# Split fp32r sums over 64 channels, and intra-chunk products of two heads as one group, in a hybrid RWKV-7 and attention layer

## The chip, the cores and the metric

The kernel runs on one core of a Trainium2 chip. The metric is the device time of one execution in microseconds. The five engines work through instruction queues of their own, each in a fixed order: PE (TensorE, matrix products), DVE (VectorE), ACT (ScalarE), POOL (GpSimd) and SP (which here issues the transfers).

## The reference

One layer of a streaming encoder, on 1,024 frames of a prompt and 64 frames of a second sequence with a cache of 256 (D_MODEL 1024, 8 RWKV heads and 8 attention heads of 64 channels):

```python
h = _rms_norm(x, norm1_g) * (1 + sc1[:, None]) + sh1[:, None]
proj = h @ w_in
...
kk = kk / jnp.maximum(jnp.linalg.norm(kk, axis=-1, keepdims=True), 1e-12)
...
y, s_new = _rwkv_scan(rh, _heads(decay, RWKV_HEADS), kh, vh, kk, _heads(a, RWKV_HEADS), s_prev.astype(f32))
mu = jnp.mean(y, axis=-1, keepdims=True)
var = jnp.mean(jnp.square(y - mu), axis=-1, keepdims=True)
y = ((y - mu) * lax.rsqrt(var + GN_EPS)).reshape(b, t, RWKV_WIDTH) * gn_g + gn_b
bonus = (jnp.sum(rh * kh * r_k, axis=-1, keepdims=True) * vh).reshape(b, t, RWKV_WIDTH)
...
q = _rms_norm(_heads(q, FOX_HEADS), fox_q_g)
kf = _rms_norm(_heads(kf, FOX_HEADS), fox_k_g)
...
mix = jnp.concatenate([y_rwkv, y_fox], axis=-1) @ w_out
x = x + gt1[:, None] * mix
...
ffn = (jax.nn.silu(h2 @ w_ffn_gate) * (h2 @ w_ffn_up)) @ w_ffn_down
```

Every norm, mean and sum over the last axis of a head is a sum over 64 channels.

## The kernel before, in words

Data lies with channels on the 128 partitions, two heads of 64 channels to a tile, and frames along the columns. The frames come in two halves: half 0 has 512 frames (8 chunks of 64), half 1 has the other 512 and the 64 of the second sequence (9 chunks, 576 columns, worked on in two pieces of 288).

For each half a table of letters (ORDER) sets in which order the work is written down. Z, Q, K and V are projections (`pmm`, lines 321 to 323: each weight and each activation is split into a high and a low part in the type fp32r, and three products are summed). D and A prepare a pair of heads j for the scan; B (rwkv_b) is the scan over its 8 or 9 chunks; N (rwkv_n) normalises the scan's result y; q and k (fox_norm) normalise the queries and keys of attention. A scheduler then fixes each engine's order, once, from dependencies and estimated times; on the chip an engine never overtakes in its queue.

A step of the scan is a chain: pR (L624) on PE, copies of it on DVE and ACT (L626, L627), pSA (L637), its negation on DVE and ACT (L638, L639), pS (L640), the new state on DVE (L644), and the next step's pR. The two pY products (L635, L645) stand beside it.

The sums over 64 channels are made by bsum (L398): the data are multiplied on PE by a 128x128 matrix with a block of ones (`bones`) or of 1/64 (`bmean`) for each head, in fp32, one product (`pbs`, L402) to a piece of 512 columns in half 0 and 288 in half 1. There are 48 calls, 24 in each half: for each pair two in A, two in N, one for q and one for k. The intra-chunk products pA (L491) multiply kb by rk for each chunk and head, 64 rows by 128 columns, four chunks to a PSUM tile of tag "ra"; a masked eviction on DVE (L493) makes At of them, from which the next steps (pg, pw, pu, lines 550 to 578) form the inverse matrices.

SBUF is handed out by tags, each with a number of buffers. `slot` without a tag takes from "ms", which has one buffer. "fx" has four: raw and squared q or k (fraw, fsq) hold two of them from their projection to the end of fox_norm.

Of the kernel before, what the change touches and what calls it, by code (L numbers as in the profile page):

```python
# [2 lines left out]

# [4 lines left out]
F32 = mybir.dt.float32  # L8
F32R = mybir.dt.float32r
BF16 = mybir.dt.bfloat16  # L10
AF = mybir.ActivationFunctionType
ALU = mybir.AluOpType
# [4 lines left out]
P = 128  # L17
# [3 lines left out]
SS = 64  # L21
# [43 lines left out]
class K:  # L65
    def __init__(self, tc, A, O):
        self.tc, self.nc, self.A, self.O = tc, tc.nc, A, O
        self.flip = 0

        self.pool_lo = False  # L70


    def consts(self):
# [39 lines left out]
    def consts2(self):  # L113
        nc, A = self.nc, self.A
        c, f = self.cpool, self.fper
        self.bones = f.tile([P, P], F32, name="bones")
        self.bmean = f.tile([P, P], F32, name="bmean")
        for t, v in ((self.bones, 1.0), (self.bmean, 1.0 / 64)):
            nc.gpsimd.memset(t, 0.0)
            nc.gpsimd.memset(t[0:64, 0:64], v)  # L120
            nc.gpsimd.memset(t[64:128, 64:128], v)
        self.tri = f.tile([P, P], F32, name="tri")
        nc.gpsimd.memset(self.tri, 1.0)
        nc.gpsimd.affine_select(out=self.tri, in_=self.tri, compare_op=ALU.is_ge, fill=0.0, base=0,
                                pattern=[[1, P]], channel_multiplier=-1)
        self.lacc = None


        self.amask = f.tile([P, 2, P], F32, name="amask")
        nc.gpsimd.memset(self.amask, 1.0)  # L130
        for h in range(2):
            am = self.amask[:, h]
            nc.gpsimd.memset(am[64 * h:64 * h + 64, 0:64], -1.0)
            for r in (0, 64):
                nc.gpsimd.affine_select(out=am[r:r + 64, 0:64], in_=am[r:r + 64, 0:64], compare_op=ALU.is_gt,
                                        fill=0.0, base=0, pattern=[[1, 64]], channel_multiplier=-1)
                nc.gpsimd.affine_select(out=am[r:r + 64, 64:128], in_=am[r:r + 64, 64:128], compare_op=ALU.is_ge,
                                        fill=0.0, base=0, pattern=[[1, 64]], channel_multiplier=-1)

        self.whi2 = [self.fper.tile([P, RW], F32R, name=f"whi{x}") for x in range(2)]
        self.wlo2 = [self.fper.tile([P, RW], F32R, name=f"wlo{x}") for x in range(2)]
        for x in range(2):
            raw = self.slot([P, RW], name="wlr")
            for r in (0, 64):
                nc.sync.dma_start(raw[r:r + 64], A["w_lora"][x])
            r = slice(64 * x, 64 * x + 64)
            nc.scalar.copy(self.whi2[x], raw)
            nc.gpsimd.memset(self.wlo2[x].bitcast(F32), 0.0)  # L150
            nc.vector.tensor_tensor(self.wlo2[x][r], raw[r], self.whi2[x][r].bitcast(F32), op=ALU.subtract)

        self.fb = c.tile([P, 8], F32, name="fb")
        nc.sync.dma_start(self.fb, A["fox_f_b"].to_broadcast([P, 8]))
        self.fsel = c.tile([P, 8], F32, name="fsel")
        nc.vector.tensor_reduce(self.fsel, self.ident.rearrange("p (i b) -> p b i", i=4)[:, 0:8], axis=AX.X, op=ALU.add)
        self.wg = self.fper.tile([P, RW], F32, name="wg")
        nc.sync.dma_start(self.wg, A["w_gate_up"])
        self.carry = c.tile([P, 14], F32, name="carry")
        self.ns = c.tile([P, 28], F32, name="ns")  # L160

        self.state = [f.tile([P, 64], F32, name=f"state{j}") for j in range(4)]
        for t in self.state:
            nc.gpsimd.memset(t, 0.0)

        self.cmul = f.tile([P, 320], F32, name="cmul")
        nc.gpsimd.memset(self.cmul, 1.0)
        nc.gpsimd.memset(self.cmul.rearrange("p (c t) -> p c t", t=64)[:, :, 0:1], 0.0)
# [227 lines left out]
            evac(ps[:, 0:n], off, n)  # L396

    def bsum(self, hf, w, x, evac, tag):  # L398
        nc = self.nc
        for off, n in hf.chunks:  # L400
            ps = self.ps([P, 512], tag=tag, name="pbs")
            nc.tensor.matmul(ps[:, 0:n], w, x[:, off:off + n], start=True, stop=True)  # L402
            evac(ps[:, 0:n], off, n)

    def split_lora(self, hf, z):

# [8 lines left out]
    def rwkv_d(self, hf, j, zl):  # L415

        nc, vc = self.nc, self.vc
        n, nch = hf.n, hf.nch
        col = lambda base: vc[:, base + j:base + j + 1]
        ch = lambda t: t[:, 0:n].rearrange("p (c t) -> p c t", t=64)  # L420
        sw, a = self.slot(name="sw", tag="sa"), self.slot(name="a", tag="sa")
        for off, m in hf.chunks:

            ps = [self.ps([P, 512], tag="ra", name="plora") for _ in range(2)]
            for x in range(2):
                nc.tensor.matmul(ps[x][:, 0:m], self.whi2[x][:, j * P:(j + 1) * P], zl[:, x, off:off + m], start=True,
                                 stop=False)
            for x in range(2):
                nc.tensor.matmul(ps[x][:, 0:m], self.wlo2[x][:, j * P:(j + 1) * P], zl[:, x, off:off + m], start=False,
                                 stop=True)  # L430
            for x, (dst, base) in enumerate(((sw, V_W0), (a, V_A0))):
                nc.vector.tensor_scalar(dst[:, off:off + m], ps[x][:, 0:m], col(base), -43.0, op0=ALU.add, op1=ALU.max)
        self.sigm(sw[:, 0:n], 1.0)
        self.sigm(a[:, 0:n], 1.0)
        cum = self.slot(name="cum", tag="sa")
        for o in range(0, n, 320):
            m = min(320, n - o)
            nc.vector.tensor_tensor_scan(cum[:, o:o + m], self.cmul[:, 0:m], sw[:, o:o + m], 0.0, ALU.mult, ALU.add)
        pp = self.pp
        nc.scalar.activation(pp[:, 0:nch, 1:65], ch(cum), AF.Exp, scale=-KAPPA)  # L440
        nc.scalar.activation(cum[:, 0:n], cum[:, 0:n], AF.Exp, scale=KAPPA)
        return a, cum

    def rwkv_a(self, hf, j, z, d):

        nc, vc, O = self.nc, self.vc, self.O
        n, nch = hf.n, hf.nch
        ng = 2 * nch
        col = lambda base: vc[:, base + j:base + j + 1]
# [34 lines left out]
        for c in range(0, nch, 4):  # L484
            m = min(4, nch - c)

            pa = [self.ps([P, 4, P], tag="ra", name="pA") for _ in range(2)]
            for i in range(m):
                for h in range(2):
                    hp = slice(64 * h, 64 * h + 64)  # L490
                    nc.tensor.matmul(pa[h][:, i], kb[hp, c + i], rk[hp, c + i], start=True, stop=True)  # L491
            for h in range(2):
                nc.vector.tensor_tensor(At[:, c:c + m, :, h], pa[h][:, 0:m].rearrange("p i (x t) -> p i x t", x=2),  # L493
                                        self.amask[:, h:h + 1].rearrange("p o (x t) -> p o x t", x=2)
                                        .to_broadcast([P, m, 2, 64]), op=ALU.mult)

        nb = 2 * ng
        dm = self.dpool.tile([2, ng, 2, 16, 16], F32, tag="dm", name="dm")
# [13 lines left out]
        for s in range(15):  # L512
            m = 15 - s
# [172 lines left out]
    def logf(self, hf):  # L686
# [58 lines left out]
            nc.gpsimd.tensor_copy(keep, acc)  # L745
            self.lacc = keep

        q4 = self.fpool.tile([P, 7, 4, 8], F32, tag="lq", name="lq")
        hi = self.fpool.tile([P, 7, 2, 8], F32R, tag="lh", name="lh")
        for i, _, _, _, _ in order:  # L750
            nc.vector.tensor_copy(hi[:, i, 0], pl[:, i])
# [85 lines left out]
    def by_tokens(self, hf, j, src):  # L837
        nc = self.nc
        pt = self.ps([P, 4, P], tag="fx", name="pkv")
        for i in range(4):  # L840
            nc.tensor.transpose(pt[:, i], src[:, i * P:(i + 1) * P], self.ident)
        dst, ds_ = self.slot([P, 4, P], name="tok", tag="fx"), None
        nc.scalar.copy(dst, pt)
        nc.sync.dma_start(self.O["fox_v"][j, :, 4 * hf.i:4 * hf.i + 4], dst)
        if hf.smp:
            pt = self.ps([SS, P], tag="fx", name="pkvs")
            nc.tensor.transpose(pt, src[:, 512:576], self.ident)
            ds_ = self.fpool.tile([SS, P], F32, tag="toks", name="toks")
            nc.scalar.copy(ds_, pt)
            nc.sync.dma_start(self.O["fox_v"][j, 0:SS, 8], ds_)  # L850
        return dst, ds_
# [518 lines left out]
    def run(self):  # L1370
        tc, nc, A, O = self.tc, self.nc, self.A, self.O
        halves = [Half(0), Half(1)]
        with ExitStack() as top:
# [22 lines left out]
            self.cmid = E(mid, "cmid")  # L1396
            self.consts()
            self.spool = MultiPool({"mrow": E(mid, "smrow", 2), "mred": E(mid, "smred", 2)})
            self.spool.pools.update({"ms": E(mid, "sms", 1)})
            hst = top.enter_context(ExitStack())  # L1400
            hp = E(hst, "hpool", side="right")
            self.hhi = hp.tile([P, KT, 576], F32R, name="hhi")
# [48 lines left out]
            RP = lambda p, tags: MultiPool({t: E(rws, p + t, b) for t, b in tags})  # L1451
            self.rpool.pools.update(RP("r", (("pp", 1), ("pb", 2), ("mb", 1), ("wb", 1), ("tb", 1), ("xl", 1))).pools)
            self.spool.pools.update(RP("s", (("sa", 4),)).pools)
            self.fpool = FP("f", (("toks", 1), ("lfu", 1), ("lfe", 1), ("lfw", 1), ("lacc", 2), ("lq", 1), ("lh", 1)))
            self.spool.pools.update(FP("s", (("fx", 4),)).pools)
            self.ops = {}

# [305 lines left out]
```

## Time and profile before

| | us |
|---|---|
| median of 3 runs (lowest to highest) | 1698.58 (1694.36 to 1699.02) |
| the profiled execution: its span | 1691.4 |
| PE busy in it | 1642.2 |
| weight loads of PE | 1438.5 |
| DVE busy | 1122.1 |
| ACT busy | 725.6 |

The page gives times of one profiled execution; its span is the time from its first instruction to its last, and the three runs were timed apart from it. Rows of a group read: line, engine, operation, tile written <- tiles read, how many records; then the busy time of the group in us and the mean of one in ns; then the idle time of the engine before it and who ended it. Rows of the timeline read: start in us, length in us, engine, line, operation, tiles, shapes, count, and in brackets how long the engine sat idle before and what released it. An fp32 product has two records (x2). Work on the projections, the scan and the norms lies between about 67 and 730 us, attention of half 0 from there to 945, then half 1, the feed-forward from 985 to 1420 and its last product up to the end.

### The profile page before, as it was taken

Reading aid. Unit: us, or ns where it says so; the run is one execution under the profiler, and the core shown is the slowest. Engines: PE = TensorE matmul, PEld = TensorE weight load, DVE = VectorE, ACT = ScalarE, POOL = GpSimd, SP = SyncE. Lnnn points to the kernel's source line nnn. Section 1 sums busy time; section 2 is a strip of 40 time slices with the busy share of each in tenths; the row PEclk is TensorE's granted clock in tenths of the full one; section 3 lists DMA queues with packets and bytes.
Section 4 is the critical chain, followed back from the end, with each engine's and each line's share of the span. In section 5 each row is a group of like instructions: output and inputs, shape, how many; then the busy total and the mean of one; then the engine's idle time right before and its main releaser. Section 6 shows DMA issues by size and latency. Waiting matters only on the chain.

```text
span 1691.4 us, 33224 instructions
## 1 busy us (share of the span) xinstructions
PE 1642.2 (97%) x12891; PEld 1438.5 (85%) x12891; DVE 1122.1 (66%) x2561; ACT 725.6 (43%) x1524; POOL 184.7 (11%) x412
## 2 busy tenths in 40 slices
PE   6999999999999999989999999999999999999999
PEld 3776776788888888667889899999999999999998
DVE  6776676757867655886887985555555556545545
ACT  4535364653545345775776633333333333111210
POOL 2102230222121212201220000000000000000000
PEclk9999999999999999998999999999999999999999
DMA  8544447541233344466564532222222215423313
GB/s 310 163 129 132 141 136 201 175 124 33 72 85 85 81 136 115 144 203 177 156 194 153 178 121 78 77 77 77 78 77 77 77 65 178 146 87 97 97 38 125
DMA packets 133580, 207.08 MB, mean 122 GB/s; under 512 B 62126, under 2 KB 70350, under 8 KB 133422
## 3 DMA queue, kind: packets, MB, share of 16 engines
q1 hardware_dynamic: 133422, 204.95, 39.6%
q8 instruction: 102, 1.67, 0.4%
q14 instruction: 56, 0.46, 0.1%
HBM read 157.65 MB, written 47.25 MB: 121 GB/s over the span
## 4 chain that ended last, share of the span: by engine, by line
PE 85%; ACT 5%; DVE 5%; DMA 4%; issue 2%; SPq 0%; ACTq 0%; DVEq 0%
PE pd L1302 15%; PE pfe L1187 8%; PE pfc L1187 7%; PE pfa L1187 7%; PE pmm L321 5%; PE pmm L322 5%; PE pmm L323 5%; PE pfb L1187 4%; PE pbs L402 2%; PE pav L989 2%; PE ppt L967 2%; PE pA L491 2%; PE po L321 2%; PE po L322 2%; PE po L323 2%
## 5 line engine op out<-in xcount | busy, mean ns | idle before, releaser
L321 PE MATMUL pmm<-hhi,whi 128*128 128x288 f32 (+1 forms) x624 | 218.2, 350 | 2.4 <-ACT pb L344 1.4
L322 PE MATMUL pmm<-hlo,whi 128*128 128x288 f32 (+1 forms) x624 | 216.4, 347 | 0.7 <-DVE hlo L299 0.7
L323 PE MATMUL pmm<-hhi,wlo 128*128 128x288 f32 (+1 forms) x624 | 214.7, 344 | 0.6 <-DVE wlo L243 0.6
L239 ACT CAST whi<-wraw 128x1024 fp32r<-128x1024 f32 (+2 forms) x116 | 99.2, 855 | 210.0 <-PE pd L1302 163.6
L1302 PE MATMUL pd<-al,whi 128*128 128x512 f32 (+1 forms) x528 | 172.4, 326 | 0.0
L1302 PE MATMUL pd<-ah,whi 128*128 128x512 f32 (+1 forms) x528 | 172.2, 326 | 0.0
L1302 PE MATMUL pd<-ah,wlo 128*128 128x512 f32 (+1 forms) x528 | 172.2, 326 | 0.0
L1306 DVE SCALAR_TENSOR_TENSOR x1t<-pd,mod,x1t 128x512 f32<-128x512 f32 x192 | 91.2, 498 | 106.6 <-PE pd L1302 105.9
L321 PEld LDWEIGHTS pmm<-hhi,whi 128*128 128x128 f32 x624 | 118.4, 190 | 13.9 <-ACT pb L344 2.0
L322 PEld LDWEIGHTS pmm<-hlo,whi 128*128 128x128 f32 x624 | 118.2, 189 | 10.9 <-DVE hlo L299 1.4
L323 PEld LDWEIGHTS pmm<-hhi,wlo 128*128 128x128 f32 x624 | 118.1, 189 | 10.7 <-issue 1.7
L243 DVE TENSOR_TENSOR wlo<-wraw,whi 128x1024 fp32r<-128x1024 f32 (+2 forms) x108 | 104.2, 964 | 19.5 <-ACT whi L239 18.7
L1302 PEld LDWEIGHTS pd<-ah,whi 128*128 128x128 f32 x528 | 99.1, 188 | 7.1
L1302 PEld LDWEIGHTS pd<-ah,wlo 128*128 128x128 f32 x528 | 99.1, 188 | 7.1
L1302 PEld LDWEIGHTS pd<-al,whi 128*128 128x128 f32 x528 | 99.1, 188 | 6.9
L1187 PE MATMUL pfc<-hh,hS 128*128 128x256 f32 (+1 forms) x352 | 101.8, 289 | 1.1 <-ACT hh L1089 1.1
L1187 PE MATMUL pfa<-hh,whi 128*128 128x256 f32 (+1 forms) x352 | 102.1, 290 | 0.0
L1187 PE MATMUL pfc<-hh,lS 128*128 128x256 f32 (+1 forms) x352 | 101.8, 289 | 0.0
L1187 PE MATMUL pfa<-hl,whi 128*128 128x256 f32 (+1 forms) x352 | 101.6, 289 | 0.0
L1187 PE MATMUL pfa<-hh,wlo 128*128 128x256 f32 (+1 forms) x352 | 101.5, 289 | 0.0
L1187 PE MATMUL pfc<-hl,hS 128*128 128x256 f32 (+1 forms) x352 | 100.7, 286 | 0.0
L631 POOL TENSOR_SCALAR sd<-sv,pc 64x64 f32<-64x64 f32 x136 | 77.0, 566 | 181.3 <-DVE sv L644 157.7
(368 smaller groups left out, 4380.7 us busy)
## 6 DMA issues: line engine op xcount, KB each, us to landing
wraw<-in_w_in_dram SPq DMA_DIRECT2D x52, 512.0 KB
wada<-in_w_ada_dram SPq DMA_DIRECT2D x48, 512.0 KB
as<-actscr SPq DMA_DIRECT2D x22, 544.0 KB
wraw<-in_w_gate_dram SPq DMA_DIRECT2D x22, 512.0 KB
wraw<-in_w_up_dram SPq DMA_DIRECT2D x22, 512.0 KB
wraw<-in_w_down_dram SPq DMA_DIRECT2D x40, 256.0 KB
wraw<-in_w_out_dram SPq DMA_DIRECT2D x16, 512.0 KB
actscr<-sg SPq DMA_DIRECT2D x22, 288.0 KB
```

Source lines behind the costliest of these rows:

```text
L239: nc.scalar.copy(hi, src)
L243: eng.tensor_tensor(lo, src, hi.bitcast(F32), op=ALU.subtract)
L321: nc.tensor.matmul(ps[0:M, 0:n], whi[:, k, 0:M], xhi[:, k, off:off + n], start=(k == 0), stop=False)
L322: nc.tensor.matmul(ps[0:M, 0:n], whi[:, k, 0:M], xlo[:, k, off:off + n], start=False, stop=False)
L323: nc.tensor.matmul(ps[0:M, 0:n], wlo[:, k, 0:M], xhi[:, k, off:off + n], start=False, stop=(k == kt - 1))
L402: nc.tensor.matmul(ps[:, 0:n], w, x[:, off:off + n], start=True, stop=True)
L491: nc.tensor.matmul(pa[h][:, i], kb[hp, c + i], rk[hp, c + i], start=True, stop=True)
L631: nc.gpsimd.tensor_scalar(sd[hsl[h]], sv[hsl[h], c, h], pc[hsl[h], c], None, op0=ALU.mult)
L967: nc.tensor.transpose(pt[0:rows, b - b0, t * P:t * P + qn], p[0:qn, pc:pc + rows], self.ident[0:qn, 0:qn])
L1187: nc.tensor.matmul(ps, l[:, k], r[:, s, k], start=(first and k == 0 and y == 0), stop=(k == 3 and y == 2), skip_group_check=True)
L1302: nc.tensor.matmul(ps[:, 0:n], w[:, i], x[:, t:t + n], start=(i == 0 and y == 0), stop=(i == len(fs) - 1 and y == 2))
L1306: nc.vector.scalar_tensor_tensor(dst, ps[:, so - off:so - off + l], self.mod[:, 40 + o, b:b + 1], dst, op0=ALU.mult, op1=ALU.add)
```

## The change

Two edits, and the tiles that go with them:

- **bsum** takes pieces of 256 columns in half 0 and 288 in half 1. For each, ACT casts the data to fp32r (`bhl`, part 0), DVE subtracts the cast from the data (part 1), two fp32r products are summed in the same PSUM tile, and the piece is evicted as before. `bones` and `bmean` are fp32r now. That makes 96 pieces, 96 casts, 96 subtractions and 192 products in place of 72 fp32 products.
- **pA**: the products of the two heads of a group of four chunks are issued in turn, each tied behind the one before it (issue_after) and at high priority. The first also waits for the last two instructions noted in `freed`, which are the last evictions of "ra" tiles.
- "ms" has three buffers in place of one; q4 and the 64-frame value tile come from other pools now.

```diff
-        self.bones = f.tile([P, P], F32, name="bones")
-        self.bmean = f.tile([P, P], F32, name="bmean")
-        for t, v in ((self.bones, 1.0), (self.bmean, 1.0 / 64)):
-            nc.gpsimd.memset(t, 0.0)
-            nc.gpsimd.memset(t[0:64, 0:64], v)
-            nc.gpsimd.memset(t[64:128, 64:128], v)
+        self.bones = f.tile([P, P], F32R, name="bones")
+        self.bmean = f.tile([P, P], F32R, name="bmean")
+        blk = self.slot([P, P], name="blk")
+        nc.gpsimd.memset(blk, 0.0)
+        nc.gpsimd.memset(blk[0:64, 0:64], 1.0)
+        nc.gpsimd.memset(blk[64:128, 64:128], 1.0)
+        nc.vector.tensor_copy(self.bones, blk)
+        nc.vector.tensor_scalar(self.bmean, blk, 1.0 / 64, None, op0=ALU.mult)
...
     def bsum(self, hf, w, x, evac, tag):
-        nc = self.nc
-        for off, n in hf.chunks:
+
+        nc = self.nc
+        m = 288 if hf.smp else 256
+        for off, n in ((o, m) for o in range(0, hf.n, m)):
+            hl = self.slot([P, 2, 288], F32R, name="bhl")[:, :, 0:n]
+            nc.scalar.copy(hl[:, 0], x[:, off:off + n])
+            nc.vector.tensor_tensor(hl[:, 1], x[:, off:off + n], hl[:, 0].bitcast(F32), op=ALU.subtract)
             ps = self.ps([P, 512], tag=tag, name="pbs")
-            nc.tensor.matmul(ps[:, 0:n], w, x[:, off:off + n], start=True, stop=True)
-            evac(ps[:, 0:n], off, n)
+            for i in range(2):
+                nc.tensor.matmul(ps[:, 0:n], w, hl[:, i], start=(i == 0), stop=(i == 1))
+            out = evac(ps[:, 0:n], off, n)
+            if tag == "ra":
+                self.freed.append(out)
+
+    def after(self, ins, others):
+
+        for o in others:
+            self.tc.add_manual_dep(ins.ins, o.ins.name, mybir.DependencyInfo(
+                mybir.DependencyClass.Sync, mybir.DependencyReason.DATA), reason="after")
...
             for x, (dst, base) in enumerate(((sw, V_W0), (a, V_A0))):
-                nc.vector.tensor_scalar(dst[:, off:off + m], ps[x][:, 0:m], col(base), -43.0, op0=ALU.add, op1=ALU.max)
+                self.freed.append(nc.vector.tensor_scalar(dst[:, off:off + m], ps[x][:, 0:m], col(base), -43.0, op0=ALU.add,
+                                                          op1=ALU.max))
...
             pa = [self.ps([P, 4, P], tag="ra", name="pA") for _ in range(2)]
+            mm = None
             for i in range(m):
                 for h in range(2):
                     hp = slice(64 * h, 64 * h + 64)
-                    nc.tensor.matmul(pa[h][:, i], kb[hp, c + i], rk[hp, c + i], start=True, stop=True)
+                    with self.tc.high_priority(), self.tc.issue_after(mm.ins) if mm else nullcontext():
+                        new = nc.tensor.matmul(pa[h][:, i], kb[hp, c + i], rk[hp, c + i], start=True, stop=True)
+                    if mm is None:
+                        self.after(new, self.freed[-2:])
+                    mm = new
             for h in range(2):
-                nc.vector.tensor_tensor(At[:, c:c + m, :, h], pa[h][:, 0:m].rearrange("p i (x t) -> p i x t", x=2),
+                self.freed.append(nc.vector.tensor_tensor(At[:, c:c + m, :, h], pa[h][:, 0:m].rearrange("p i (x t) -> p i x t", x=2),
                                         self.amask[:, h:h + 1].rearrange("p o (x t) -> p o x t", x=2)
-                                        .to_broadcast([P, m, 2, 64]), op=ALU.mult)
+                                        .to_broadcast([P, m, 2, 64]), op=ALU.mult))
...
-        q4 = self.fpool.tile([P, 7, 4, 8], F32, tag="lq", name="lq")
+        q4 = self.slot([P, 7, 4, 8], name="lq")
...
-            ds_ = self.fpool.tile([SS, P], F32, tag="toks", name="toks")
+            ds_ = self.slot([P, P], name="toks", tag="mrow")[0:SS]
...
-            self.spool.pools.update({"ms": E(mid, "sms", 1)})
+            self.spool.pools.update({"ms": E(mid, "sms", 3)})
...
-            self.fpool = FP("f", (("toks", 1), ("lfu", 1), ("lfe", 1), ("lfw", 1), ("lacc", 2), ("lq", 1), ("lh", 1)))
+            self.fpool = FP("f", (("lfu", 1), ("lfe", 1), ("lfw", 1), ("lacc", 2), ("lh", 1)))
```

With both kernels built, the fixed order of an engine can be compared. (Lines after L398 stand some 23 later in the changed kernel: 624 is 647 and so on.)

The first place is on PE, the intra-chunk products of pair 0 in half 0; `pada` is a product of the adaLN modulation, which is spread through this stage. Before:

```order
L491 MATMUL pA_999<-rk_982,kb_983 128x128 x4
L191 MATMUL pada_1211<-wada_1209,ct_141 32x128
L491 MATMUL pA_1000<-rk_982,kb_983 128x128 x4
L191 MATMUL pada_1211<-wada_1209,ct_141 32x128
L491 MATMUL pA_1011<-rk_982,kb_983 128x128 x4
L191 MATMUL pada_1211<-wada_1209,ct_141 32x128 x6
L321 MATMUL pmm_1232<-hhi_175,whi_1228 128x512
L491 MATMUL pA_1012<-rk_982,kb_983 128x128 x4
```

After:

```order
L411 MATMUL pbs_1010<-bhl_1007,bones_628 128x256
L194 MATMUL pada_1172<-wada_1170,ct_141 32x128 x3
L511 MATMUL pA_1015<-rk_987,kb_988 128x128
L511 MATMUL pA_1016<-rk_987,kb_988 128x128
L511 MATMUL pA_1015<-rk_987,kb_988 128x128
L511 MATMUL pA_1016<-rk_987,kb_988 128x128
L511 MATMUL pA_1015<-rk_987,kb_988 128x128
L511 MATMUL pA_1016<-rk_987,kb_988 128x128
L511 MATMUL pA_1015<-rk_987,kb_988 128x128
L511 MATMUL pA_1016<-rk_987,kb_988 128x128
L202 MATMUL pada_1172<-ident_130,mrow_1181 128x128
L324 MATMUL pmm_1193<-hhi_175,whi_1189 128x512
```

A block of four products of each head, with other work between, has become eight products in turn.

The second place is on PE too, inside the scan of pair 2 in half 1 (pR, pY, pSA, pS, pY is one step). Before:

```order
L321 MATMUL pmm<-hhi,whi 128x288
L624 MATMUL pR<-sv,At 128x128
L635 MATMUL pY<-rk,sv 128x128
L322 MATMUL pmm<-hlo,whi 128x288
L323 MATMUL pmm<-hhi,wlo 128x288
L321 MATMUL pmm<-hhi,whi 128x288
L322 MATMUL pmm<-hlo,whi 128x288
L323 MATMUL pmm<-hhi,wlo 128x288
L321 MATMUL pmm<-hhi,whi 128x288
L637 MATMUL pSA<-R,inv_692 128x64
L322 MATMUL pmm<-hlo,whi 128x288
L323 MATMUL pmm<-hhi,wlo 128x288
```

After, where the second step of that scan begins:

```order
L326 MATMUL pmm<-hhi,wlo 128x288
L663 MATMUL pS<-sv,kb 128x128
L668 MATMUL pY<-At,sv 128x128
L647 MATMUL pR<-sv,At 128x128
L658 MATMUL pY<-rk,sv 128x128
L660 MATMUL pSA<-R,inv_686 128x64
L663 MATMUL pS<-sv,kb 128x128
L668 MATMUL pY<-At,sv 128x128
L647 MATMUL pR<-sv,At 128x128
L658 MATMUL pY<-rk,sv 128x128
L660 MATMUL pSA<-R,inv_686 128x64
L663 MATMUL pS<-sv,kb 128x128
```

Projections stood between the products of a step; from the second step on, the steps follow each other to the ninth with nothing between.

The third place is on ACT around the end of the same scan: y is what the scan yields (L650, now L673), gsq the squared y in N, fsq the squared q or k. Before:

```order
L650 COPY y_7507<-pY_7519 64x256
L627 COPY R_7587<-pR_7585 64x64
L639 ACTIVATE sv_7478<-pSA_7596 64x64
L627 COPY R_7606<-pR_7604 64x64
L239 CAST whi_8519<-wraw_8517 128x1024
L639 ACTIVATE sv_7478<-pSA_7614 64x64
L785 COPY fraw_7938<-pmm_7973 128x288
L786 ACTIVATE fsq_7939<-pmm_7973 128x288
L795 ACTIVATE fsq_7939<-pbs_8000,eps_n_154 128x288
L795 ACTIVATE fsq_7939<-pbs_8003,eps_n_154 128x288
```

After:

```order
L673 COPY y_7893<-pY_7980 64x256
L650 COPY R_8053<-pR_8051 64x64
L407 CAST bhl_8223<-y_7893 128x288
L662 ACTIVATE sv_7864<-pSA_8062 64x64
L673 COPY y_7893<-pY_8060 64x64
L407 CAST bhl_8230<-y_7893 128x288
L687 ACTIVATE gsq_8237<-y_7893 128x576
L407 CAST bhl_8239<-gsq_8237 128x288
L407 CAST bhl_8246<-gsq_8237 128x288
L407 CAST bhl_8263<-fsq_8162 128x288
L689 ACTIVATE gsq_8237<-pbs_8242,eps_g_156 128x288
```

The logarithm of a q or k sum (L795) stood between two steps of the scan; now the cast of fsq stands behind the four casts of y and gsq, which stand at the scan's end. The numbers of bhl rise from row to row.

3 lines of the change are left out of this document (2 added, 1 removed).

## The prediction

> **What bounds the kernel now.** I read the page's totals first, then the chain that ended last, then the windows by stage, and only then single rows.
>
> ```profile
> span 1691.4 us, 33224 instructions
> PE 1642.2 (97%) x12891; PEld 1438.5 (85%) x12891; DVE 1122.1 (66%) x2561; ACT 725.6 (43%) x1524; POOL 184.7 (11%) x412
> PE 85%; ACT 5%; DVE 5%; DMA 4%; issue 2%; SPq 0%; ACTq 0%; DVEq 0%
> ```
>
> PE is busy for 97% of the span and makes 85% of the chain; DVE follows far behind. The three runs lie 3.0 to 7.6 us above this span (1694.36 to 1699.02), the median 7.2. I make the sum against the span of 1691.4 and add 7.2 at the end. Everything that the change touches lies between 67 and 730 us, so the three windows there matter (columns: sum, then busy time and count of PE, PEld, DVE, ACT, POOL, granted clock, DMA share, GB/s); the window of the feed-forward is for comparison.
>
> ```profile
> 67.00:370.00 303.00, 295.53 (x2569) 220.25 (x2567) 216.68 (x573) 152.87 (x320) 63.30 (x125) 0.99 0.51 147
> 370.00:600.00 230.00, 225.12 (x2102) 194.34 (x2100) 168.01 (x466) 109.09 (x257) 51.69 (x111) 1.00 0.28 75
> 600.00:730.00 130.00, 122.12 (x1043) 99.42 (x1043) 83.94 (x270) 78.97 (x228) 30.86 (x72) 0.99 0.47 129
> 985.00:1420.00 435.00, 435.00 (x3457) 434.88 (x3456) 260.54 (x500) 132.76 (x248) 0.00 (x0) 1.00 0.25 81
> PE pS L640 <- ACT sv L639: 3.5, 8, 0.8
> ```
>
> In the first three PE is busy 642.8 of 663 us (295.53 + 225.12 + 122.12): at most 20 us of idle time in the whole stage, DVE 468.6 (71%), ACT 340.9 (51%). The dearest wait of PE, quoted last from the table of waits, is 3.5 us in eight places. The stage is full because the scan (rwkv_b), a chain across three engines, has projections (pmm) standing between its products. So work taken off PE is worth its time only while PE still has something to do at each place; that is the question here.
>
> **The 64-channel sums.** 48 sums, 24 in each half: 24 fp32 products of 512 columns and 48 of 288.
>
> ```profile
> 82.61 1.12 PE L402 MATMUL pbs<-z,bones 128*128 128x512 f32 x2
> 83.67 1.16 PE L491 MATMUL pA<-rk,kb 64*128 64x128 f32 x8
> 84.75 0.41 PE L191 MATMUL pada<-wada,ct 128*32 128x128 f32 x2
> 477.95 1.13 PE L402 MATMUL pbs<-sq,bones 128*128 128x288 f32 x4
> 478.92 0.65 PE L402 MATMUL pbs<-fsq,bones 128*128 128x288 f32 x2
> ```
>
> From start to next start a 512-column product takes 1.06 us (82.61 to 83.67), and two of 288 take 0.97, so 0.49 each: 24 x 1.06 + 48 x 0.49 = 49 us. Afterwards there are 192 fp32r products of 256 or 288 columns. The feed-forward window is a row of 3,457 such products back to back, 435.00 / 3457 = 0.126 us each: 24 us. Each of the 96 pairs also enters between other work: between nothing and one more product (0.126, 12 us in all); I take half, 6. Saved: 49 - 30 = **19 us** (13 to 25).
>
> What it adds: 96 casts on ACT and 96 subtractions on DVE of 256 or 288 columns.
>
> ```profile
> L981 DVE TENSOR_TENSOR ptl<-ppt,pth 128x256 fp32r<-128x256 f32 x32 | 13.3, 416 | 1.3 <-ACT pth L980 0.8
> L980 ACT CAST pth<-ppt 128x256 fp32r<-128x256 f32 x32 | 11.9, 371 | 9.6 <-PE pav L989 7.0 <-PE ppt L967 2.4
> ```
>
> At these durations ACT gets 36 us more (377 of 663, 57%) and DVE 40 (509, 77%). Neither becomes the fullest engine, so I cost this load at nothing by itself; the cover is PE's own queue of projections, and where that cover is gone the cast and the subtraction stand in the chain at 0.8 us a chunk. The 24 more evictions of half 0 are two of 256 for one of 512 and are covered in the same way. The three fewer memsets on POOL at the start stand beside the adaLN work: nothing.
>
> **The products of two heads.** pA has 136 products (272 records).
>
> ```profile
> L491 PE MATMUL pA<-rk,kb 64*128 64x128 f32 x272 | 34.0, 288 | 0.5 <-DVE At L493 0.5
> 522.92 1.17 PE L491 MATMUL pA<-rk,kb 64*128 64x128 f32 x16
> 524.02 0.75 PE L395 MATMUL plora<-z,wg 128*128 128x288 f32 x2
> ```
>
> Four products of one head took 1.08 us (83.67 to 84.75); where eight already stood in turn, head by head, they took 1.10 together (522.92 to 524.02). Each head takes 64 of the array's 128 rows (the 64*128 in the row), and the two ran beside each other. So 16 groups of eight cost 16 x 1.10 = 17.6, and four pairs of the ninth chunk 4 x 0.4 = 1.6 (an estimate between one product's 0.27 and two's 0.54). Saved: 34.0 - 19.2 = 15, less about 1 for ends that overlapped others: **14 us** (10 to 17). The added wait, of the first of the eight for the evictions of the last two "ra" tiles, holds the projections queued behind it on PE; it lasts one masked eviction at most, and the order puts adaLN or sum products ahead of it: nothing.
>
> Together PE gets 33 us less work (23 to 42).
>
> **What moves.** The operands of the split sums, bhl, share a ring of three, and the order shows that it is given out in the order in which the program is written: the numbers of bhl only rise. A q/k sum that is written behind rwkv_n's sums now stands behind them on ACT, and those need y, which the scan yields at its end. Until then the fx slots of that q or k are held, and with them the next projections. This is the second place of the order shown above: in half 1, pair 2, seven steps of the scan stand on PE with nothing between them, where before 8 to 21 projection products stood in each. I counted all 60 gaps from one pR to the next within a scan in both orders: before, every gap has filler; now **18 have none, or one row**: five in pair 0 of half 1, seven in pair 2, four in pair 3, two in half 0.
>
> What a bare step costs is read off a step whose chain was tight:
>
> ```profile
> 558.51 0.39 PE L624 MATMUL pR<-sv,At 128*128 128x128 f32 x2
> 558.73 0.39 PE L635 MATMUL pY<-rk,sv 128*128 128x128 f32 x2
> 558.93 0.22 DVE L626 COPY R<-pR 64x64 f32<-64x64 f32 x1 [0.64 <-PE pR L624]
> 559.18 0.21 ACT L627 COPY R<-pR 64x64 f32<-64x64 f32 x1 [0.73 <-DVE R L626]
> 559.44 0.43 PE L637 MATMUL pSA<-R,inv 128*128 128x64 f32 x2
> 559.99 0.22 DVE L638 TENSOR_SCALAR sv<-pSA 64x64 f32<-64x64 f32 x1 [0.84 <-PE pSA L637]
> 560.30 0.22 ACT L639 ACTIVATE sv<-pSA 64x64 f32<-64x64 f32 x1 [0.91 <-DVE sv L638]
> 560.57 0.49 PE L640 MATMUL pS<-sv,kb 128*128 128x128 f32 x2
> 560.89 0.39 PE L645 MATMUL pY<-At,sv 128*128 128x128 f32 x2
> 561.10 0.60 DVE L644 SCALAR_TENSOR_TENSOR sv<-pS,pc,sd 64x64 f32<-64x64 f32 x2 [0.89 <-PE pS L640]
> 561.84 0.46 PE L624 MATMUL pR<-sv,At 128*128 128x128 f32 x2
> ```
>
> DVE and ACT stood idle before every link, so 3.33 us (558.51 to 561.84) is the chain itself. PE's own part is five products at 0.14 to 0.32 from start to start (0.22 for pR, 0.32 for pS), some 1.1 to 1.2. Idle: 2.1 a step, at most 2.25, at least 1.85 if the handovers to PE get 0.1 shorter at each of three places. 18 x 2.1 = **38 us** (33 to 41).
>
> There are also stretches with no projection outside the steps: the preamble of pair 1 in half 0 (pg to pR), the turn from half 0 to half 1, and the sums and preambles that follow the scans of pairs 0 and 2 in half 1. Two rows each bound them:
>
> ```profile
> 599.10 0.76 PE L550 MATMUL pg<-gt,At 32*32 32x32 f32 x36
> 613.91 0.46 PE L624 MATMUL pR<-sv,At 128*128 128x128 f32 x2 [0.24 <-ACT sv L605]
> 718.68 0.75 PE L402 MATMUL pbs<-y,bmean 128*128 128x288 f32 x2 [0.22 <-DVE y L661]
> 720.23 0.67 ACT L664 ACTIVATE gsq<-y 128x576 f32<-128x576 f32 x1
> 720.95 0.75 PE L402 MATMUL pbs<-gsq,bmean 128*128 128x288 f32 x2
> 721.74 0.50 ACT L666 ACTIVATE gsq<-pbs,eps_g 128x288 f32<-128x288 f32 x1
> ```
>
> pg to pR took 14.8 us; its own products on PE come to some 8 or 9 (an estimate), so some 6 idle. rwkv_n's two sums took 3.6 (718.68 to 722.24), and get four times 0.8 of cast and subtraction: 6.8, nearly all idle on PE. Four places at 7: **28 us**, between 2 each (8, if most of it stands beside the sums of the q/k) and 11 each (45, if preamble and sums follow one after the other).
>
> Of before's own idle time in the stage, 20 us, the 3.5 us of pS lay in scan steps and go in part with the steps that are now counted whole; I take 2 off. Net: -33 + 38 + 28 - 2 = +31. 1691.4 + 31 + 7.2 = **1729.6**.
>
> **The rivals.**
> - Faster: the bare steps are short. In the step above ACT's copy of R and of sv starts only behind DVE's; each costs 0.45 in a row. If the two ran side by side with nothing else queued, a step would take 2.4, its idle time 1.3: 18 x 1.3 = 23, with 8 for the other stretches 31, against 42 saved at most: 1691.4 - 11 + 7.2 = 1688. It decides from a step under 2.4 us. Against it: each ACT row names DVE's as its releaser. 0.09.
> - No difference: saving 36 (above the middle), bare steps 30, stretches 8: about 1700. 0.09.
> - The pairs do not run beside each other (the change doesn't do what it says), because the waits between them keep the heads apart: 14 us not saved, 1743. The row of sixteen records at 522.92 speaks against it. 0.07.
> - DVE becomes what PE waits for: 96 x 0.8 = 77 us of cast and subtraction, of which half stands alone in the chain, 39 more: 1768. DVE at 77% speaks against it, its fixed order for it. 0.07.
> - PE has headroom that its busy time hides: a product's recorded end is modelled, and in the first window weight loads fill only 73% (220.25 of 303) where the feed-forward has 434.88 of 435. If work taken off PE is worth only that share, the 33 us become 24 and the time 1739. Against it: the fp32 products in the rows above follow each other without a gap, and start to start, not by recorded ends, they give the 49 us. 0.05. [...]
>
> **How the numbers follow.** The forecast has 0.63, from -42 + 33 + 8 = -1 (1698) to -23 + 41 + 45 = +63 (1762). The range takes in that, the pairs and the headroom, and reaches down to 1690 for half of the faster case: 1690 to 1764, leaving out some 0.12. A measurement of this kernel tells 0.3% from no change (1693.5 and 1703.7). Faster 0.09; same 0.09; slower 0.82, all else.
>
> **What would show it.** In the changed kernel's profile: fp32r sums with a mean below 0.3 us and pA groups of eight in 1.1 us (the saving); in half 1, runs of five and seven scan steps 3.0 to 3.3 us apart with PE idle between them and waits of pR, pSA and pS on DVE and ACT of some 35 us in sum, where now they are below 10; DVE below 80%. It would be wrong if those steps came 2.4 us apart, if PE's busy time didn't fall by 23 to 42, or if the idle time arose elsewhere, above all in waits of projections for weights.

## The result, and the profile after

The changed kernel takes **1865.67 us** (median of 4, 1860.67 to 1872.28) against 1696.86 before (median of four runs, the three of the table above among them): ratio 1.1003, 95% interval 1.0986 to 1.102. It is 169 us slower where I had forecast 31. The direction was right and the size was wrong by a factor of five; the range ended at 1764.

The page of the changed kernel, the lines that were quoted of before and the row of the clock:

```profile
span 1860.6 us, 33596 instructions
PE 1704.1 (92%) x12939; PEld 1491.0 (80%) x12939; DVE 1164.5 (63%) x2671; ACT 760.7 (41%) x1632; POOL 182.3 (10%) x409
PEclk9999679769997899588799999999999999999999
PE 78%; DVE 9%; ACT 7%; DMA 3%; issue 3%; SPq 0%; DVEq 0%; ACTq 0%
```

The third line is the one to read. Each digit is the clock that PE was granted in a fortieth of the span, in tenths of full speed (9 is 90% or more). The same row of before:

```profile
PEclk9999999999999999998999999999999999999999
```

Before, the row is nines with a single 8, and the mean is 0.992; now it falls to 5, 6, 7 and 8 again and again in the first half, and the mean is 0.924. PE's busy time *rose* by 62 us (1642.2 to 1704.1) although the change takes work off it: products at the lower clock took longer (a group of eight pA 2.08 us at 0.5 and 1.16 at 1.0). The prediction had named this as a sign of being wrong (a fall of 23 to 42 us was forecast).

The trace records the clock as a series of stretches, at either 1.0 or 0.5, and nothing between. That lets the span of any kernel here be split into three parts that add up: PE's idle time (span less PE's busy time); the surcharge of the half clock (half of the time in which PE was busy at 0.5); and the rest, which is PE's work as it would be at full clock. The surcharge is an estimate: it counts everything that PE did at 0.5 as lasting twice as long, and one step measured at both clocks further down lasts 1.91 times as long (8.96 against 4.69 us).

| kernel | span | idle | surcharge | work at full clock |
|---|---|---|---|---|
| before | 1691.4 | 49.2 | 13.3 | 1628.9 |
| the change | 1860.6 | 156.5 | 103.7 | 1600.3 |
| difference | +169.2 | +107.3 | +90.4 | -28.6 |

For the change: clock 0.924 over 1860.6 us is 283 us at half clock; PE was idle in 76 of them and busy in 207, and half of that is 104.

Where the time lies, by the first and last pR of each scan: the eight scans together take 254 us before and 256 now. The stretches between them grow from 310 to 446 us, and what follows the last pR from 979 to 1021; the first pR comes 12 us earlier. The worst stretch lies between the scans of pairs 0 and 1 in half 0, 32.5 us before and 100.2 now. The windows of that stretch, of before (one row) and then of the change (from 179.4 to 242 us of it):

```profile
179.00:211.50 32.50, 31.75 (x374) 23.01 (x374) 21.92 (x49) 12.02 (x27) 6.66 (x11) 1.00 0.47 146
```

```profile
179.40:187.00 7.60, 0.43 (x2) 0.00 (x0) 7.41 (x12) 1.91 (x4) 0.00 (x0) 0.70 0.27 98
187.00:199.60 12.60, 10.56 (x48) 7.81 (x48) 9.39 (x20) 5.10 (x12) 0.00 (x0) 0.50 0.05 7
199.60:210.10 10.50, 0.04 (x1) 0.00 (x0) 9.13 (x23) 5.64 (x11) 0.65 (x1) 0.50 0.28 71
210.10:220.00 9.90, 7.99 (x44) 5.43 (x45) 8.42 (x34) 2.27 (x7) 0.00 (x0) 0.50 0.21 46
220.00:242.00 22.00, 20.25 (x123) 15.06 (x123) 8.59 (x19) 9.77 (x17) 1.13 (x5) 1.00 0.21 41
```

PE does next to nothing for 7.6 us, works at half clock for 12.6, does nothing for 10.5, works at half clock again, and is at full clock only when projections come back. The rows behind its waits in the timeline of the change:

```profile
115.12 0.60 ACT L809 ACTIVATE fsq<-pmm 128x512 f32<-128x512 f32 x1
185.76 0.75 DVE L496 SCALAR_TENSOR_TENSOR z<-z,vc 128x512 f32<-128x512 f32 x1
186.54 0.71 ACT L407 CAST bhl<-z 128x256 fp32r<-128x256 f32 x2 [5.69 <-DVE z L496]
187.00 1.59 PE L411 MATMUL pbs<-bhl,bones 128*128 128x256 f32 x5 [7.17 <-ACT bhl L407]
188.14 0.41 ACT L407 CAST bhl<-fsq 128x256 fp32r<-128x256 f32 x1 [0.57 <-PE pbs L411]
189.13 2.08 PE L511 MATMUL pA<-rk,kb 64*128 64x128 f32 x16 [0.53 <-DVE bon L498]
210.16 0.63 PE L194 MATMUL pada<-wada,ct 128*32 128x128 f32 x2 [10.52 <-ACT fsq L809]
```

The cast of z waits for the end of rwkv_a's chain on DVE; only behind it come the casts of fsq, the squared q or k, which had been ready since 115.7 us. That is the ring in program order, as forecast, but behind the sums of the preparation, where I had counted on those of the scan's result. The last row is the second wait: a product stands behind the eviction of the next q or k projection (fsq). And the group of eight pA lasts 2.08 us, where the row of sixteen records quoted in the prediction lasts 1.17.

The scan steps without a projection are there too (17 in the trace have no other product between them, or one), but ten of them are 4.33 us long, not 3.3:

```profile
739.80 0.77 PE L647 MATMUL pR<-sv,At 128*128 128x128 f32 x2 [0.35 <-DVE sv L667]
740.68 0.22 DVE L649 COPY R<-pR 64x64 f32<-64x64 f32 x1 [1.02 <-PE pR L647]
741.19 0.69 PE L660 MATMUL pSA<-R,inv 128*128 128x64 f32 x2 [0.19 <-ACT R L650]
742.57 0.80 PE L663 MATMUL pS<-sv,kb 128*128 128x128 f32 x2 [0.69 <-ACT sv L662]
744.15 0.77 PE L647 MATMUL pR<-sv,At 128*128 128x128 f32 x2 [0.36 <-DVE sv L667]
```

Against the step quoted in the prediction, the copies on DVE and ACT last what they did (0.22), and each product of PE lasts 0.25 to 0.4 longer: 0.77 for pR against 0.39, 0.80 for pS against 0.49. The first bare step in the scan of pair 0 of half 1 shows the same products still at full clock, which falls at 578.4 us:

```profile
574.89 0.46 PE L647 MATMUL pR<-sv,At 128*128 128x128 f32 x2 [0.17 <-DVE sv L667]
576.16 0.43 PE L660 MATMUL pSA<-R,inv 128*128 128x64 f32 x2 [0.59 <-ACT R L650]
577.44 0.49 PE L663 MATMUL pS<-sv,kb 128*128 128x128 f32 x2 [0.85 <-ACT sv L662]
```

That step takes 3.82 us. DVE, which had other work, started its copy of R and its negation 0.3 and 0.2 us later than in the step of the prediction, and without that it would be about as long as forecast; PE is idle for 1.99 us of it (forecast 2.1). The next step runs at half clock and takes 4.33.

### The profile page after: what moved, and what is told of

Same layout as the page of the kernel before. It is cut to its first block, busy times and chain, and to the rows that moved or that the text cites. A ratio compares the mean times of both kernels' runs of the same rounds, so it can differ in the third digit from the quotient of the medians.

```text
span 1860.6 us, 33596 instructions
## 1 busy us (share of the span) xinstructions
PE 1704.1 (92%) x12939; PEld 1491.0 (80%) x12939; DVE 1164.5 (63%) x2671; ACT 760.7 (41%) x1632; POOL 182.3 (10%) x409
## 4 chain that ended last, share of the span: by engine, by line
PE 78%; DVE 9%; ACT 7%; DMA 3%; issue 3%; SPq 0%; DVEq 0%; ACTq 0%
PE pd L1325 14%; PE pfe L1210 7%; PE pfc L1210 7%; PE pfa L1210 7%; PE pmm L324 5%; PE pmm L325 5%; PE pmm L326 5%; PE pfb L1210 3%; PE pav L1012 2%; PE pbs L411 2%; PE ppt L990 2%; PE pS L663 2%; PE po L324 2%; PE po L325 1%; PE po L326 1%
## 5 line engine op out<-in xcount | busy, mean ns | idle before, releaser
L324 PE MATMUL pmm<-hhi,whi 128*128 128x288 f32 (+1 forms) x624 | 222.4, 356 | 14.3 <-ACT fsq L809 5.3
L324 PEld LDWEIGHTS pmm<-hhi,whi 128*128 128x128 f32 x624 | 123.0, 197 | 27.2 <-ACT fsq L809 6.4
L325 PEld LDWEIGHTS pmm<-hlo,whi 128*128 128x128 f32 x624 | 123.1, 197 | 9.3 <-DVE hlo L302 1.1
L326 PEld LDWEIGHTS pmm<-hhi,wlo 128*128 128x128 f32 x624 | 122.5, 196 | 9.4 <-DVE wlo L246 1.1
```

Source lines behind the costliest of these rows:

```text
L324: nc.tensor.matmul(ps[0:M, 0:n], whi[:, k, 0:M], xhi[:, k, off:off + n], start=(k == 0), stop=False)
L325: nc.tensor.matmul(ps[0:M, 0:n], whi[:, k, 0:M], xlo[:, k, off:off + n], start=False, stop=False)
L326: nc.tensor.matmul(ps[0:M, 0:n], wlo[:, k, 0:M], xhi[:, k, off:off + n], start=False, stop=(k == kt - 1))
```

## The experiments

The same split for all (us, of the profiled execution; the medians and ratios stand at each run):

| kernel | span | idle | surcharge | work at full clock |
|---|---|---|---|---|
| e1: pairs, tiles moved | 1735.2 | 74.6 | 50.3 | 1610.2 |
| e2: split sums, tiles moved | 1861.0 | 148.1 | 102.3 | 1610.6 |
| e3: all, three rings by use | 1771.3 | 99.6 | 78.8 | 1592.9 |
| e4: tiles moved, nothing else | 1733.4 | 71.0 | 36.7 | 1625.7 |
| e5: pairs, no tile moved | 1691.3 | 59.4 | 18.5 | 1613.3 |
| e6: e5 without the wait | 1718.3 | 59.1 | 31.6 | 1627.6 |
| e8: all, no tile moved, q/k ring apart | 1810.6 | 125.2 | 82.5 | 1603.0 |
| e9: all, no tile moved, preparation's ring apart | 1858.0 | 133.5 | 126.7 | 1597.8 |
| e10: all, no tile moved, one buffer | 1878.6 | 160.5 | 106.8 | 1611.4 |

**Which half of the change?** Each part alone, with the tiles' moves of the change, and the whole change with rings by use:

```diff
-            hl = self.slot([P, 2, 288], F32R, name="bhl")[:, :, 0:n]
+            hl = self.slot([P, 2, 288], F32R, name="bhl", tag="b" + tag)[:, :, 0:n]
...
-            self.spool.pools.update({"ms": E(mid, "sms", 3)})
+            self.spool.pools.update({"bra": E(mid, "sbra", 1), "brb": E(mid, "sbrb", 1), "bfx": E(mid, "sbfx", 1)})
+            self.spool.alias = {"ms": "bfx"}
```

> The change with its products of two heads in turn, but the 64-channel sums as one fp32 product again (the ring of three is there, unused by sums). Theory (the ring shared by all split sums, given out in program order, lets PE run dry, and PE's clock falls with it): without split sums there is no such ring; the fixed order has two scan steps without filler where the change has 18; time 1675 to 1700 us, clock 0.98 or more. Rival (the pairs, at high priority and with an added wait, block PE): the loss stays with the pairs, 1800 us or more, clock about 0.92. Expected: theory, about 1690.

> The change with its split sums, but the products of two heads issued as before (no high priority, no wait, no order between them). Theory (ring): 16 scan steps without filler in the fixed order; the loss stays, 1850 to 1885 us, clock 0.91 to 0.93. Rival (the pairs): 1700 us or less, clock 0.98 or more. Expected: theory, about 1870.

> The whole change, but the operands of the split sums come from three rings of one buffer each, by use (sums of the preparation, of the scan's result, of queries and keys), in place of one ring of three for all. Theory (order of the shared ring): a sum of queries no longer waits behind one that waits for the scan or for the preparation's chain on DVE; two scan steps without filler; 1670 to 1720 us, clock 0.97 or more. Rival (the cast and the subtraction themselves, or the load of DVE and ACT, are what PE waits for): 96 casts and subtractions are as before, so it stays above 1800 us. Expected: theory, about 1700.

Measured: pairs only 1737.87 us (ratio 1.0244, 1.0228 to 1.0261), sums only 1867.22 (1.1016, 1.0986 to 1.1045), rings by use 1770.14 (1.043, 1.0408 to 1.0453). The sums, with the moved tiles, carry the loss, and taking the shared ring apart takes 96 us of it away (1866 to 1770). Both theories missed on e1: it is neither near 1690 nor 1800. e3 came out by neither of its theories: it lies 50 us above the band of the ring (1670 to 1720) and 30 below that of the casts, so the ring is the largest cause and not the only one.

**What costs 42 us in e1?** Its pairs save work (1610.2 against 1628.9), so something else costs. The tiles' moves, with the three buffers of ms, were the suspect:

```diff
-        q4 = self.fpool.tile([P, 7, 4, 8], F32, tag="lq", name="lq")
+        q4 = self.slot([P, 7, 4, 8], name="lq")
...
-            ds_ = self.fpool.tile([SS, P], F32, tag="toks", name="toks")
+            ds_ = self.slot([P, P], name="toks", tag="mrow")[0:SS]
...
-            self.spool.pools.update({"ms": E(mid, "sms", 1)})
+            self.spool.pools.update({"ms": E(mid, "sms", 3)})
```

> The kernel before with neither part of the change, only the moves of tiles that go with it: the pool ms with three buffers, q4 in it, the 64-frame value tile in mrow. The engines' work is the same. Theory A (the order of before is one that a tuned table gives, and moving q4 alone makes the scheduler give another, with more runs of small products and no projection among them): slower than before, 1720 to 1745 us, clock about 0.97, like the pairs with these moves (1738). Rival B (the pairs themselves cost those 42 us): 1690 to 1702 us, clock 0.99. Expected: A, about 1730.

> The kernel before with the products of two heads in turn as the change has them (high priority, wait, order), fp32 sums, and no tile moved. Theory A: 14 us of PE's work less and few new runs of small products: 1680 to 1700 us, clock 0.98 or more. Rival B (the pairs cost): about 1738 us, as with the moves. Expected: A, about 1690.

> As the run before it, without the added wait for the last evictions (the first product of a group waits only for its own tile). If the wait costs nothing, the same time within 5 us as with it; the fixed order has slightly fewer runs without projections: 1675 to 1695 us, expected 1684.

Measured: tiles only 1733.52 us (1.0212, 1.0192 to 1.0231); pairs with no tile moved 1696.22 (0.9998, 0.9986 to 1.001); without the wait 1718.34 (1.0122, 1.0101 to 1.0143). Moving two tiles and giving ms three buffers costs 37 us. The two traces hold the same instructions (12,891 records on PE) in another order, with 22 us more idle time and 23 more surcharge. The pairs on the old places do what they say. The rows of the group, of before, of e5 and of e6:

```profile
L491 PE MATMUL pA<-rk,kb 64*128 64x128 f32 x272 | 34.0, 288 | 0.5 <-DVE At L493 0.5
```

```profile
L503 PE MATMUL pA<-rk,kb 64*128 64x128 f32 x272 | 21.5, 296 | 1.0 <-DVE At L508 0.9
```

```profile
L503 PE MATMUL pA<-rk,kb 64*128 64x128 f32 x272 | 30.1, 293 | 1.2 <-DVE At L506 0.7 <-DVE bon L490 0.2
```

12.5 us less busy time, and 15.6 less work by the split; 10 more of idle time and 5 of surcharge take it all back. The wait, which I had costed at nothing, earns: without it the first product of a group goes off alone (0.42 us, then the other seven in 1.09), and 8.6 us of what pA's rows had saved are lost. My expectation for e6 was wrong. Its profiled execution is 27.0 us longer than that of e5: 14.3 are work, those 8.6 among them, and 13.1 surcharge; that these come from its other order is argued, not tested.

**Which sharing of the ring?** No tile moved. e8 and e9 have two buffers, and what differs is who shares with whom; e10 has one buffer for all.

```diff
+            hl = self.slot([P, 2, 288], F32R, name="bhl", tag="bx" if tag in ('fx',) else "ms")[:, :, 0:n]
...
+            self.spool.pools.update({"ms": E(mid, "sms", 1), "bx": E(mid, "sbx", 1)})
```

(e9 has `('ra',)` there.)

> The whole change with no tile moved: ms keeps its one buffer and serves the sums of the preparation and of the scan's result; the sums of queries and keys get one buffer of their own. Theory A (what costs is that sums of queries and keys queue behind sums that wait for the scan or for the preparation's chain, so that projections stop): most of the loss goes, 1690 to 1750 us, slow-clock time about 100 us; expected 1715. Rival (fewer buffers, or split sums as such, cost): 1800 us or more.

> As the run before it, with as many buffers, but the buffer apart serves the sums of the preparation; queries and keys still share one with the scan's result. Theory A: the loss stays, 1830 to 1890 us, expected 1860. Rival (any second ring helps, by its number of buffers): as the run before it.

> The whole change with no tile moved and one buffer for all split sums. Theory A: the number of buffers hardly matters where they are given out in one order, 1840 to 1890 us, as the change with three (1866). If the moved tiles add a cost of their own beside the ring (37 us when alone), this is 1830 us or less; if three buffers helped, above 1890.

Measured: queries and keys apart 1817.8 us (1.0712, 1.0691 to 1.0733), preparation apart 1856.58 (1.0944, 1.0926 to 1.0962), one buffer for all 1882.87 (1.1102, 1.1083 to 1.1121). The order of the three is as expected: one buffer or three in one line make little difference (1883 and 1866, with the moved tiles in the second), and it helps more to free the queries and keys (65 us) than the preparation (26). But e8 missed its band by 68 us and lies in that of its rival (fewer buffers, or split sums as such, cost: 1800 or more). In e8 preparation and scan's result still queue behind each other, which e3 removes too; e3, with the same casts, is 48 us faster, but it also has one buffer more. So I read the sharing as a graded cost, not one culprit, and what the split sums cost without any sharing stays open.

**Is it the clock?** Products without use were put into the scan steps of pairs 0, 2 and 3 of half 1; first twelve at one place (e7), then in all three waits of a step (e11):

```diff
+            idle(pS, mm, 8)
...
+            idle(pS, mm, 12)
...
+            idle(pa2, mm, 12)
```

where `idle(ps, after, k)` issues k products of `bones` and `bmean`, in order, into a tile that is overwritten or no longer read.

> The whole change, plus twelve idle products of 128 columns in each scan step of pairs 0, 2 and 3 of half 1 (written to a tile that the next product overwrites), some 0.7 us of work a step, 18 us in all. Theory C (a bare step is long because PE's clock falls to half when a stretch holds too little work): the clock stays full in these scans, bare steps fall from 4.33 to 3.3 to 3.5 us, and the time does not rise: 1845 to 1866 us. Rival D (a bare step's chain takes 4.33 us whatever the clock, for its links on DVE and ACT): steps stay at 4.3 or grow, the time rises by up to 18 us, 1866 to 1885. Expected: C, about 1855.

> The whole change, plus idle fp32r products of 128 columns in the gaps of each scan step of pairs 0, 2 and 3 of half 1: eight behind the first pY, twelve behind pSA, twelve behind the second pY, each group in a wait of PE, none of its results used (some 1.8 us of work a step at full clock, put where PE otherwise waits). 21 steps there have no projection. Theory C (a bare step takes 4.33 us because PE's clock is halved there, and it is halved because too little work fills the 3.4 us before): the clock comes back to full within the scans, bare steps take 3.3 to 3.6 us. Rival D (the step's 4.33 us are its links on DVE and ACT, and the clock follows from other causes): steps of 4.3 us or more, at half clock, and the added products lengthen them to 5 us or more. Expected: C. The time says little (projections leave these scans, some of the added work delays others): 1840 to 1890 us.

Both were executed once. e7 could not decide: 1896.48 us; its products stood ahead of pSA, lengthened the chain (4.16 us a step at full clock) and still let the clock fall, and then a step of the same rows took 6.34. e11 (1928.64 us, above the 1840 to 1890 expected) tells more than I asked of it. From the second step on, its steps have the same rows in all three scans, none with a projection. The scan of pair 0 fell to half clock in its second step and stayed there to its end; those of pairs 2 and 3 kept the full clock throughout. Windows of e11, first within the scan of pair 0, then the whole scan of pair 2:

```profile
572.00:633.60 61.60, 60.29 (x284) 60.25 (x283) 8.57 (x33) 3.71 (x16) 7.86 (x18) 0.51 0.06 9
766.80:807.10 40.30, 39.00 (x344) 38.50 (x344) 13.86 (x59) 5.66 (x25) 7.60 (x18) 1.00 0.27 65
```

and the same two products with their fillers, from the timeline, pair 0 and then pair 2:

```profile
621.20 0.73 PE L672 MATMUL pS<-sv,kb 128*128 128x128 f32 x2
622.01 2.80 PE L664 MATMUL pSA<-bmean,bones 128*128 128x128 f32 x12
...
795.91 0.43 PE L672 MATMUL pS<-sv,kb 128*128 128x128 f32 x2
796.32 1.53 PE L664 MATMUL pSA<-bmean,bones 128*128 128x128 f32 x12
```

A step takes 8.96 us at half clock and 4.69 at full, for the same instructions. So the clock alone nearly doubled a step in which PE is what counts (1.91 times), and in pairs 2 and 3 the scans with the added work kept the full clock where the change without it ran at half clock for 25.5 of 34.0 and 15.5 of 36.1 us. The first half of theory C is shown by these steps and by the two in the scan of pair 0 of the change above: the long step is PE's clock, not the links on DVE and ACT. The second half, that more work in the waits keeps the clock up, held in two scans of three; that the clock comes back was wrong for pair 0. Its "3.3 to 3.6 us" was wrong too, since the fillers took more than the waits had room for.

## Why the prediction was wrong, point by point

- **PE's work.** Forecast 33 us less; the split gives 28.6. The pairs were forecast at 14 and measured at 15.6 (e5), the sums at 19 and 18.3 (e2, with the tiles moved). Right; only the mean below 0.3 us that I had named for the split products did not show (0.38 to 0.49, part of it at half clock).
- **The order.** 18 steps without filler were read correctly off the order, and the ring was the right cause: rings by use take 96 us of 169 away (e3).
- **Idle time.** Forecast +64 (38 + 28 - 2); measured +107. By the first and last pR of each scan, 24.5 of it lie in the scans, 65.3 between them and 17.5 ahead of the first and behind the last. The steps were priced too high: the 17 in the trace hold 22 us of idle time, not 38, since at half clock PE's own products fill more of a step (1.22 us idle in one of 4.33). Their waits, 36.9 us for pR, pSA and pS against some 35 forecast, agree by luck in part: steps with filler have waits as well. The term "four places at 7 us" was sized too low: I took the preamble in the stretch between pairs 0 and 1 of half 0 for one of them, and that stretch alone has 33.8 us of idle time (100.2 less 66.4 busy), 7 us of it behind the cast at the end of rwkv_a's chain on DVE and 10.5 behind ACT's eviction of a q/k projection. The bare steps did not lengthen the scans as I had it (254 to 256 us in sum), since by the split 47 us of work left them.
- **The clock.** This is the step that failed: I priced idle time at its own length and let PE's own work run at full clock, since the windows of before showed 0.99 to 1.00. The surcharge of 90 us has no term in the sum at all; 24 of it lie in the scans and 57 between them. The 3.33 us step became 4.33, and three groups of eight pA lasted 2.08 us in place of 1.17. The trace of before held a warning that I passed over: its clock falls to half five times, 27.3 us in all, and the mean of its window from 730 to 945 us is 0.97. That it stayed full elsewhere because projections were never away for long is argued, not tested.
- **The tiles.** The moves of q4 and of the value tile, with the buffers of ms, weren't in the sum. Alone they cost 37 us (e4), by the order, with no instruction added.
- **The rivals.** None was right. DVE didn't become the bound: its share fell (66 to 63%), and PE's waits for bhl are 19.8 us in sum, the largest of its waits up to 950 us but a small part of the loss (from the table of waits):

```profile
PE pbs L411 <- ACT bhl L407: 19.8, 9, 7.2
PE pS L663 <- ACT sv L662: 19.3, 28, 1.7
PE pR L647 <- DVE sv L667: 9.7, 20, 1.7
PE pSA L660 <- ACT R L650: 7.9, 22, 1.2
```

What stays open: how much of e3's remaining 74 us is the moved tiles (37 alone) and how much the casts. The two need not add: e10, with no tile moved, is not faster than the change (1883 against 1866). The worst stretch has both in it: between the scans of pairs 0 and 1 of half 0 lie 64.2 us in e4, which has no split sums, 55.9 in e3 and 100.2 in the change. Open too is all that moves the clock beyond what the last section shows.

## What to carry to other kernels

Idle time on a full PE can cost more than its length: here 107 us of it came with 90 of surcharge. In these traces the clock fell after 68 of 69 windows of 3.41 us in which PE was busy for less than half of the time: where the sum leaves such a window, price both the wait and the work that follows at half clock (here a bare step of 4.33 us in place of 3.82). A ring that is shared by users that wait for different things is handed out in the order of the program, and the slowest of them holds up the rest; give each its own. Where a scheduler makes the order from a tuned table, run the change's side edits alone: here they cost 37 us with no work added, more than either part was meant to save.

## What the runs showed of the hardware

The clock record of all these kernels knows 0.5 and 1.0 only, in stretches that are multiples of 3.41 us (3.4, 6.8, 10.2, 17.1 in the change). What PE did ahead of a fall or a return can be read by laying the record over PE's rows. All thirteen traces, cut at the record's own steps into windows of 3.41 us, hold 69 full-clock windows in which PE was busy for less than half of the time, and after 68 of them the clock fell; from half to six tenths it fell after 42 of 62, above eight tenths after 25 of 5,649. In none of the clock's 175 returns was the window before less than 82% busy. Bare steps make such low windows by themselves: the one above at full clock leaves PE idle for 1.99 of 3.82 us. These are the windows that end where the three scans of half 1 in the change fall to half clock (pairs 0, 2 and 3; PE is busy for 51, 34 and 47% of them):

```profile
575.00:578.40 3.40, 1.72 (x10) 1.20 (x10) 2.41 (x7) 1.31 (x4) 0.71 (x2) 1.00 0.53 51
732.00:735.40 3.40, 1.15 (x6) 0.82 (x6) 2.67 (x14) 0.42 (x2) 1.07 (x2) 1.00 0.48 153
820.70:824.10 3.40, 1.60 (x13) 1.23 (x11) 3.04 (x6) 1.04 (x4) 2.65 (x3) 1.00 0.63 176
```

The clock also fell behind a window in which PE was busy, as two windows of e1 show, each as long as one step of the record:

```profile
207.50:210.90 3.40, 3.08 (x88) 2.53 (x89) 3.10 (x12) 2.02 (x7) 1.17 (x3) 1.00 0.29 98
210.90:214.30 3.40, 3.40 (x46) 2.47 (x46) 3.19 (x9) 2.02 (x4) 1.69 (x3) 0.50 0.75 187
```

PE was busy for 3.08 of 3.40 us, with 88 products, and the clock fell behind it. In the change the clock fell at 308.7 us behind a window in which PE was busy for 3.14 of 3.40 us; 86 of its 94 products were of 32x32. And in e11 PE was busy for 60.29 of 61.60 us at half clock and did not get it back, nearly all with products of 128 columns (284 products, 283 weight loads); in the change it came back at 220.0 us, behind a window in which PE was busy for 3.40 of 3.40 us and projections of 512 columns ran again from 218.5. What stood ahead of the fall in e11 can be read: the fall in the scan of pair 0 follows on the first of these two windows (PE busy for 54% of it), and the second (68%) is the least busy one of the scan of pair 2, which kept its clock:

```profile
569.40:572.80 3.40, 1.85 (x15) 1.60 (x14) 2.99 (x14) 0.00 (x0) 0.93 (x2) 1.00 0.37 136
770.80:774.20 3.40, 2.31 (x21) 2.18 (x21) 2.86 (x14) 0.22 (x1) 0.35 (x1) 1.00 0.04 4
```

So the same rows ran at two clocks, each of which lasted to the end of its scan; why 60 us of recorded work did not end the half clock, the runs don't show.
